# Up projections of three feed-forward blocks: from eight full products to seven of half size

## Chip, core and metric

One NeuronCore of one Trainium2 chip runs the whole program. The metric is the device time of one execution in microseconds (us); the kernel before has a median of 2261.13 us over 3 runs (2261.12 to 2262.95). In the profile PE is TensorE (its weight loads are listed apart, as PEld), DVE is VectorE, ACT is ScalarE, POOL is GpSimd, and SP is the queue that issues most transfers.

## What is computed

Two transformer blocks on 512 tokens of width 1024, in float32. Three feed-forward layers (two in the first block, one in the second) have width 2816 = 22 tiles of 128, and the change concerns these:

```python
def swiglu(h, w1, w3, w2):
    return (jax.nn.silu(h @ w1) * (h @ w3)) @ w2

x = x + 0.5 * swiglu(rms_norm(x, norm_ffn1[l]), ffn1_w1[l], ffn1_w3[l], ffn1_w2[l])
...
x = x + 0.5 * swiglu(rms_norm(x, norm_ffn2[l]), ffn2_w1[l], ffn2_w3[l], ffn2_w2[l])
...
h = rmsnorm(x, g_pre_ffn[l])
gu = h @ w_ffn_in[l]
gate, up = gu[..., :D_FF_2], gu[..., D_FF_2:]
x = x + rmsnorm((jax.nn.silu(gate) * up) @ w_ffn_down[l], g_post_ffn[l])
```

Between them stand retention, differential attention, attention over two memories, an mLSTM and a sparse attention, which the change leaves as they are.

## The kernel before, in words

**Precision.** Every float32 operand is split in two exact parts, hi and lo, of the type fp32r: ACT casts to hi (`copy_hi`, L93, or with a gain L94) and DVE subtracts to get lo (`lo`, L98, with a gain L99). A product is three matmuls (`mm3`): hi with hi, hi with lo, lo with hi, all recorded on L109.

**Weights.** `Stream` holds all weights in the order of their use. It loads one [128, 1024] tile ahead on the SP queue into one of four raw buffers (L146), splits it on ACT and DVE, and keeps `AHEAD` = 4 split tiles in front of the one in use. The split tiles, the residual and all large operands come from one pool of 41 buffers of 4 KB a partition (`q`).

**Residual and norm.** The residual x stands transposed, 8 tiles of [128 features, 512 tokens]. As each tile d is finished, `next_x` splits it with the norm's gain (ACT L94, DVE L99) and POOL squares it and adds it up (`Norm.add`, L222 and L226). 1/rms of each token comes later (`Norm.finish`: sums on PE, a power on POOL L251, a broadcast on PE L258 on) and multiplies the results, not the operands.

**Up phase** (`ffn_up`). For each of 22 tiles f the gate and the up weight (key order gate, up) each take 8 chunks of the width times 3 matmuls of 512 columns. `evac` takes the two results out of PSUM: DVE multiplies gate by 1/rms (L287), ACT applies silu (L288), DVE multiplies up by 1/rms (L290) and by the gate (L291), and the result is split (L93, L98). In the third block (`second_mix`) the residual becomes ready in two halves of 256 tokens (`resid`, `resid2`), and the first two tiles f are computed half by half.

**Down phase.** `ffn_down` goes output tile by output tile: 22 chunks times 3 matmuls of 512 columns. The third block's is `ffn_out`, with the tokens on the partitions.

The kernel is written in a layer that traces instructions and puts them in order for each engine by a planner; every engine then works through its own queue in that order, with semaphores between them. Lines that the steps below touch: L93, L94, L98, L99 (splits), L109 (matmul), L146 (weight load), L215 (sum of squares in the third block), L222, L226 (sums of squares), L251 (power), L287 to L291 (`evac`), L1651, L1716, L1725 (residual adds).

## Time and profile before

| | |
|---|---|
| median of 3 runs | 2261.13 us |
| span of the profiled execution | 2260.1 us |
| PE busy (matmuls) | 2229.0 us, 99% |
| PEld busy (weight loads, beside PE) | 1846.7 us, 82% |
| DVE busy | 1261.5 us, 56% |
| ACT busy | 850.9 us, 38% |
| POOL busy | 340.9 us, 15% |
| share of the chain that ended last: PE, DVE, ACT, POOL | 89%, 5%, 2%, 1% |
| bytes read and written | 224.9 MB, mean 100 GB/s |

The profile is of one execution, whose span runs from the first to the last instruction. The "chain that ended last" is followed back from the last instruction, at each step to what released it. A matmul's busy time holds its way through the array and overlaps the next one's, so what one costs is read from a long run of equal ones, as length by count. In the timeline, neighbours of one kind are merged into one row with their count.

### The profile page before, as it was taken

Reading aid. Unit: us, or ns where it says so; the run is one execution under the profiler, and the core shown is the slowest. Engines: PE = TensorE matmul, PEld = TensorE weight load, DVE = VectorE, ACT = ScalarE, POOL = GpSimd, SP = SyncE. Lnnn points to the kernel's source line nnn. Section 1 sums busy time; section 2 is a strip of 40 time slices with the busy share of each in tenths; the row PEclk is TensorE's granted clock in tenths of the full one; section 3 lists DMA queues with packets and bytes.
Section 4 is the critical chain, followed back from the end, with each engine's and each line's share of the span. In section 5 each row is a group of like instructions: output and inputs, shape, how many; then the busy total and the mean of one; then the engine's idle time right before and its main releaser. Section 6 shows DMA issues by size and latency. Waiting matters only on the chain.

```text
span 2260.1 us, 27814 instructions
## 1 busy us (share of the span) xinstructions
PE 2229.0 (99%) x10730; PEld 1846.7 (82%) x10730; DVE 1261.5 (56%) x2063; ACT 850.9 (38%) x1483; POOL 340.9 (15%) x392
## 2 busy tenths in 40 slices
PE   8999999999999999999999999999999999999998
PEld 6888888888888888888888878887777798888887
DVE  7444434556866655444345955736888757544422
ACT  4222223545344523222223543315666643332320
POOL 3000011301233030000230000213334104000000
PEclk9999999999999999999999999999999999999999
DMA  5332324122333322333224132531111451222321
GB/s 173 104 101 94 102 79 137 53 94 80 125 123 103 103 94 98 105 96 96 94 93 147 58 107 93 173 121 58 57 47 57 147 180 57 94 94 94 128 87 38
DMA packets 73292, 224.92 MB, mean 100 GB/s; under 512 B 8388, under 2 KB 11204, under 8 KB 73160
## 3 DMA queue, kind: packets, MB, share of 16 engines
q1 hardware_dynamic: 72584, 222.10, 30.5%
q8 instruction: 84, 1.38, 0.2%
q10 hardware_dynamic: 576, 1.05, 0.1%
q14 instruction: 48, 0.39, 0.1%
HBM read 210.01 MB, written 13.11 MB: 99 GB/s over the span
## 4 chain that ended last, share of the span: by engine, by line
PE 89%; DVE 5%; ACT 2%; issue 2%; POOL 1%; DMA 1%; SPq 0%; DVEq 0%; POOLq 0%; ACTq 0%
PE ps L109 87%; PE ps L112 2%; DVE q L98 1%; ACT q L1456 1%; POOL hr L251 1%; DVE nx L1454 1%; DVE q L99 0%; ACT q L93 0%; DMA q<-in_xT_dram 0%; DVE q L1354 0%; DVE hn L424 0%; POOL q L1461 0%; ACT q L885 0%; DMA raw<-in_w_k_dram 0%; DVE b L428 0%
## 5 line engine op out<-in xcount | busy, mean ns | idle before, releaser
L109 PE MATMUL ps<-q,q 128*128 128x512 f32 (+3 forms) x9744 | 2160.7, 382 | 13.1 <-ACT q L94 6.2
L109 PEld LDWEIGHTS ps<-q,q 128*128 128x128 f32 x9744 | 1743.2, 189 | 349.5 <-issue 6.6
L98 DVE TENSOR_TENSOR q<-raw,q 128x1024 fp32r<-128x1024 f32 (+2 forms) x381 | 471.3, 1260 | 145.1 <-ACT q L93 71.7
L93 ACT CAST q<-raw 128x1024 fp32r<-128x1024 f32 (+2 forms) x381 | 372.1, 1008 | 168.0 <-PE ps L109 90.6
L93 ACT CAST q<-b 128x512 fp32r<-128x512 f32 (+2 forms) x94 | 56.7, 613 | 362.3 <-DVE b L291 316.2
L222 POOL TENSOR_TENSOR b<-q 128x512 f32<-128x512 f32 (+1 forms) x56 | 56.0, 1003 | 764.8 <-DVE q L1651 324.6
L290 DVE TENSOR_TENSOR b<-ps,b 128x512 f32<-128x512 f32 x44 | 30.4, 690 | 163.8 <-PE ps L109 163.8
L98 DVE TENSOR_TENSOR q<-b,q 128x512 fp32r<-128x512 f32 (+2 forms) x94 | 64.6, 695 | 63.6 <-ACT q L93 62.9
L226 POOL TENSOR_TENSOR b<-b,b 128x512 f32<-128x512 f32 (+1 forms) x70 | 95.2, 1365 | 4.2
L1461 POOL TENSOR_SCALAR q<-q,nr 128x128 f32<-128x128 f32 (+3 forms) x128 | 71.9, 568 | 143.4 <-DVE nr L1459 116.2
L1456 ACT ACTIVATE q<-ps,nx 128x128 f32<-128x128 f32 (+3 forms) x128 | 67.4, 531 | 56.2 <-DVE nx L1454 31.0
L94 ACT ACTIVATE q<-q,gains 128x512 fp32r<-128x512 f32 (+1 forms) x48 | 30.3, 650 | 152.4 <-DVE q L1651 71.8
L112 PE MATMUL ps<-ident,q 128*128 128x128 f32 x512 | 80.8, 274 | 3.5 <-POOL q L1461 2.3
L98 DVE TENSOR_TENSOR q<-ps,q 128x512 fp32r<-128x512 f32 x112 | 74.1, 682 | 11.3 <-ACT q L93 10.9
L288 ACT ACTIVATE b<-b 128x512 f32<-128x512 f32 x66 | 41.2, 630 | 102.9 <-DVE b L287 102.8
L112 PEld LDWEIGHTS ps<-ident,q 128*128 128x128 f32 x512 | 61.8, 140 | 20.7 <-POOL q L1461 7.8
L93 ACT CAST q<-ps 128x512 fp32r<-128x512 f32 x112 | 62.7, 593 | 16.7 <-PE ps L109 11.6
L99 DVE SCALAR_TENSOR_TENSOR q<-q,gains,q 128x512 fp32r<-128x512 f32 (+1 forms) x48 | 47.7, 1013 | 17.4 <-ACT q L94 17.4
L1454 DVE TENSOR_REDUCE nx<-ps 128x1 f32<-128x384 f32 (+3 forms) x96 | 56.0, 583 | 0.0
L290 DVE TENSOR_TENSOR b<-ps,rb 128x512 f32<-128x512 f32 x22 | 15.2, 689 | 73.1 <-PE ps L109 73.1
L251 POOL TENSOR_TENSOR sr<-ss,mhalf 128x4 f32<-128x4 f32 x8 | 8.1, 1008 | 297.6 <-DVE ss L1088 192.9
L251 POOL TENSOR_TENSOR or<-ov,mhalf 128x1 f32<-128x1 f32 x4 | 2.2, 547 | 335.5 <-DVE ov L1994 335.5
(244 smaller groups left out, 1118.3 us busy)
## 6 DMA issues: line engine op xcount, KB each, us to landing
raw<-in_ffn_w_dram SPq DMA_DIRECT2D x118, 512.0 KB, 4.0
raw<-in_w_ffn_in_dram SPq DMA_DIRECT2D x44, 512.0 KB, 4.3
raw<-in_w_gm_dram SPq DMA_DIRECT2D x24, 512.0 KB, 3.6
raw<-in_w_ffn_down_dram SPq DMA_DIRECT2D x22, 512.0 KB, 3.6
raw<-in_w_out_dram SPq DMA_DIRECT2D x16, 512.0 KB, 4.2
raw<-in_ffn_w_dram SPq DMA_DIRECT2D x16, 384.0 KB, 3.1
raw<-in_w_mk_dram SPq DMA_DIRECT2D x8, 512.0 KB, 3.8
raw<-in_w_mv_dram SPq DMA_DIRECT2D x8, 512.0 KB, 4.5
```

The lines of the kernel that those rows point to most:

```text
L93: return self.nc.scalar.copy(out, in_)
L98: return self.nc.vector.tensor_sub(out, in_, hi.bitcast(F32))
L99: return self.nc.vector.scalar_tensor_tensor(out, in_, gain, hi.bitcast(F32), op0=ALU.mult, op1=ALU.subtract)
L109: return self.nc.tensor.matmul(out, a, b, start=start, stop=stop)
L112: return self.nc.tensor.transpose(out, in_, self.ident[:n, :n])
L222: k.nc.gpsimd.tensor_tensor(t, x, x, op=ALU.mult)
L226: k.nc.gpsimd.tensor_tensor(self.acc, self.acc, t, op=ALU.add)
L288: nc.scalar.activation(h, h, AF.Silu)
L290: nc.vector.tensor_mul(u, pb, rb)
L1454: nc.vector.tensor_reduce(mx, s.rearrange("p j b t -> p b j t"), axis=AX.XY, op=ALU.max, negate=True)
L1456: nc.scalar.activation(pr[b][:, :n], s[:, :, c, :], AF.Exp, bias=mx[:, c : c + 1], accum_out=sm[:, c : c + 1])
L1461: nc.gpsimd.tensor_scalar(pr[b][:, :n], pr[b][:, :n], r[:, c : c + 1], 1.0, op0=ALU.mult, op1=ALU.mult)
```

## The change

The matrix product of one pair of f tiles (2n, 2n+1) is cut in two along f, along the width (even and odd chunks of 128) and along the tokens (two halves of 256). Of the eight products of quarters, seven products of sums and differences take the place (Winograd's form of Strassen's scheme). Each has 4 chunks, 2 weights and 3 matmuls of 256 columns.

- Weights: POOL forms four sums of [128, 512] for each of the two weights of a pair (`_sums`); ACT and DVE split f1, both pairs of sums (1024 columns each) and the odd half of f2 (512). The raw buffers go from 4 to 6, the pool of large ones from 41 to 39.
- Moving operands (`Operands`): each pair of residual tiles is multiplied by its gain on ACT, split, and DVE forms four differences of [128, 256], which are split too.
- Products (`UpPairs`): seven for a pair, into three PSUM banks, in the order of `up_steps`. ACT copies three of the partial results out, DVE adds three others and multiplies by 1/rms, ACT applies silu, and POOL multiplies gate and up. The result is kept unsplit.
- Down: `split_g` splits the result tile by tile. `ffn_down` computes the first four output tiles side by side, chunk by chunk, with weights laid out for it, and the last four as before.
- The residual is not kept during the up phase: it is read again from memory (`xT`, `x3d`, `x6d`) by transfers on the ACT queue.

```diff
-        self.qp = pool("q", 41)
+        self.qp = pool("q", 39)
...
-    RAW = 4
+    RAW = 6
     AHEAD = 4
...
+    def _sums(self, n):
...
+        f1, f2 = (t.rearrange("p (k c) -> p k c", c=P) for t in d[key][:2])
+        t = k.q([P, 2, 4, P])
+        eng = nc.gpsimd
+        if what == "s12":
+            eng.tensor_tensor(t[:, 0], f2[:, 0::2], f2[:, 1::2], op=ALU.add)
+            eng.tensor_tensor(t[:, 1], t[:, 0], f1[:, 0::2], op=ALU.subtract)
+        else:
+            eng.tensor_tensor(t[:, 0], f1[:, 0::2], f2[:, 0::2], op=ALU.subtract)
+            eng.tensor_tensor(t[:, 1], f1[:, 1::2], d[key][2][:, 1], op=ALU.subtract)
+        d[key].append(t)
+
+    def _pair_split(self, n):
...
+        if what == "a22":
+            f2 = d[key][1].rearrange("p (k c) -> p k c", c=P)
+            t = k.q([P, 2, 4, P], F32R)
+            k.split(t[:, 0], t[:, 1], f2[:, 1::2])
+            del d[key]
+            return t[:, 0], t[:, 1]
+        t = d[key][2 if what == "s12" else 3].rearrange("p a k c -> p (a k c)")
+        h, l = k.q([P, 1024], F32R), k.q([P, 1024], F32R)
+        k.split(h, l, t)
+        return h, l
...
+    SUMS = 2
...
+    def prefetch(self, ahead):
+        while self.ns <= min(self.n + ahead, len(self.order) - 1):
+            while self.nsum <= min(self.ns + self.SUMS, len(self.order) - 1):
+                self._sums(self.nsum)
+                self.nsum += 1
+            self._split()
...
+class Operands:
...
+    def first(self, x1, x2, g1, g2):
+        k, c = self.k, slice(0, self.H)
+        b1, b2 = k.half(F32R).rearrange("p (s t) -> p s t", s=2), k.q([P, 2, S], F32R)
+        k.split(b1[:, 0], b1[:, 1], x1[:, c], g1)
+        k.split(b2[:, 0, c], b2[:, 1, c], x2[:, c], g2)
...
+    def second(self, j, x1, x2, g1, g2):
+        z1, z2 = self.gained(x1, g1), self.gained(x2, g2)
+        c = slice(self.H, S)
+        k.split(self.b2[j][:, 0, c], self.b2[j][:, 1, c], z2[:, c])
+        self.sums(z1, z2)
...
+    def both(self, x1, x2, g1, g2):
+        z1, z2 = self.gained(x1, g1), self.gained(x2, g2)
...
+        k.split(b1[:, 0], b1[:, 1], z1[:, : self.H])
+        k.split(b2[:, 0], b2[:, 1], z2)
...
+        self.sums(z1, z2)
...
+    def sums(self, z1, z2):
+        t = k.q([P, 4, H])
+        nc.vector.tensor_sub(t[:, 1], z2[:, H:], z1[:, H:])
+        nc.vector.tensor_add(t[:, 0], z1[:, :H], t[:, 1])
+        nc.vector.tensor_sub(t[:, 2:4], z2.rearrange("p (c t) -> p c t", c=2), t[:, 0:1].to_broadcast([P, 2, H]))
+        h, l = k.q([P, 4, H], F32R), k.q([P, 4, H], F32R)
+        k.split(h, l, t)
...
+def up_steps(n, early):
+    if early:
+        o = [(0, 1), (0, 2), (1, 1), (1, 2), (0, 6), (0, 5), (0, 7), (1, 6), (0, 4), (0, 3), (1, 5), (1, 7)]
     else:
+        o = [(0, 1), (0, 2), (0, 6), (0, 5), (0, 7)]
+    for i in range(2 if early else 1, n):
+        o += [(i, 1), (i - 1, 4), (i - 1, 3), (i, 2), (i, 6), (i, 5), (i, 7)]
+    return o + [(n - 1, 4), (n - 1, 3)]
...
+    LEFT = {1: ("f1", 0), 2: ("f1", 1), 3: ("s34", 1), 4: ("a22", 0), 5: ("s12", 0), 6: ("s12", 1), 7: ("s34", 0)}
+    RIGHT = {1: "b11", 2: "b21", 3: "b22", 4: "t4", 5: "t1", 6: "t2", 7: "t3"}
...
+    def out(self, f, half, z, src):
+        nc.vector.tensor_mul(z, src, self.rb[:, c].unsqueeze(1).to_broadcast([P, 2, 256]))
+        nc.scalar.activation(z[:, 0], z[:, 0], AF.Silu)
...
+        nc.gpsimd.tensor_tensor(self.g[f][:, c], z[:, 0], z[:, 1], op=ALU.mult)
+
+    def take(self, n, num):
+        if num in (1, 6, 7):
+            c[n, num] = self.copy(b[n, "x"])
+        if num == 2:
+            z = c.pop((n, 1))
+            nc.vector.tensor_add(z, z, b[n, "z"])
...
+        if num == 7:
+            z = c.pop((n, 7))
+            nc.vector.tensor_add(z, z, b[n, "y"])
+            self.out(2 * n + 1, 1, z, z)
+        if num == 4:
+            self.out(2 * n + 1, 0, k.b([P, 2, 256]), b.pop((n, "x")))
+        if num == 3:
+            z = c.pop((n, 6))
+            nc.vector.tensor_add(z, z, b.pop((n, "y")))
+            self.out(2 * n, 1, z, z)
...
+            if (n, num) == (0, 6):
+                last = self.finish()
+            if (n, num) == (0, 5):
+                self.rb = last()
...
+def split_g(k, g, f):
+    t = k.q([P, 2, S], F32R)
+    k.split(t[:, 0, :], t[:, 1, :], g[f])
+    g[f] = t
...
 def ffn_down(k, key, g):
+    ps = [k.ps() for _ in range(4)]
+    for f in range(NF):
+        if f == 0:
+            split_g(k, g, 0)
+        if f + 1 < NF:
+            split_g(k, g, f + 1)
+        if f % 2 == 0:
+            w = k.W.next((key, "a", f // 2))
+        for d in range(4):
+            c = slice((f % 2) * 512 + d * P, (f % 2) * 512 + (d + 1) * P)
+            k.mm3(ps[d], w[0][:, c], w[1][:, c], g[f][:, 0, :], g[f][:, 1, :], f == 0, f == NF - 1)
...
+    for d in range(0, KD, 2):
+        first[d // 2]()
+        next_pair(x, ops, d, G["norm_ffn1"], norm)
+    x.clear()
+    g = UpPairs(k, ("ffn1_w1", "ffn1_w3"), ops, norm.finish).run()
     for d in range(KD):
+        x.append(k.half())
+        nc.scalar.dma_start(x[d], aps["xT"][d])
```

## Rows read from the trace of the kernel before

**Rows 1.** The page: busy time by engine; shares of the chain that ended last.
```profile
PE 2229.0 (99%) x10730; PEld 1846.7 (82%) x10730; DVE 1261.5 (56%) x2063; ACT 850.9 (38%) x1483; POOL 340.9 (15%) x392
...
PE 89%; DVE 5%; ACT 2%; issue 2%; POOL 1%; DMA 1%; SPq 0%; DVEq 0%; POOLq 0%; ACTq 0%
```

**Rows 2.** Timeline of PE (start, length, operation, shapes, count): long runs of each width.
```profile
2134.76 110.55 PE L109 MATMUL ps<-q,q 128*128 128x512 f32 x487
...
1862.60 20.39 PE L109 MATMUL ps<-q,q 128*128 128x256 f32 x168
...
1891.80 13.44 PE L109 MATMUL ps<-q,q 128*128 128x256 f32 x110
```

**Rows 3.** Groups by shape (busy us, mean ns of one | idle before): weight loads.
```profile
L109 PEld LDWEIGHTS ps<-q,q 128*128 128x128 f32 x9744 | 1743.2, 189 | 349.5 <-issue 6.6 <-DVE q L99 6.5 <-ACT q L94 6.2
```

**Rows 4.** A stretch of the first up phase: PE, PEld, DVE, ACT, POOL busy, clock, DMA.
```profile
150.00:200.00 50.00, 50.00 (x222) 41.39 (x222) 24.40 (x29) 15.76 (x20) 0.00 (x0) 1.00 0.30 95
```

**Rows 5.** Groups by shape: DVE, ACT and POOL operations of the up phases and norms.
```profile
L98 DVE TENSOR_TENSOR q<-raw,q 128x1024 fp32r<-128x1024 f32 x341 | 434.2, 1294 | 131.8 <-ACT q L93 68.7 <-PE ps L109 50.5 <-issue 10.8
...
L291 DVE TENSOR_TENSOR b<-b,b 128x512 f32<-128x512 f32 x66 | 45.5, 692 | 7.0 <-ACT b L288 1.1
...
L93 ACT CAST q<-raw 128x1024 fp32r<-128x1024 f32 x341 | 348.3, 1049 | 147.8 <-PE ps L109 81.1 <-issue 17.5 <-DMA raw<-in_ffn_w_dram 13.4
...
L226 POOL TENSOR_TENSOR b<-b,b 128x512 f32<-128x512 f32 x42 | 71.7, 1715 | 2.4
...
L226 POOL TENSOR_TENSOR b<-b,b 128x256 f32<-128x256 f32 x28 | 23.5, 840 | 1.7
```

**Rows 6.** Timeline of POOL while the first residual tiles are prepared.
```profile
10.97 1.49 POOL L222 TENSOR_TENSOR b<-q 128x512 f32<-128x512 f32 x1
12.42 1.73 POOL L226 TENSOR_TENSOR b<-b,b 128x512 f32<-128x512 f32 x1
14.11 1.22 POOL L222 TENSOR_TENSOR b<-q 128x512 f32<-128x512 f32 x1
15.29 1.46 POOL L226 TENSOR_TENSOR b<-b,b 128x512 f32<-128x512 f32 x1
...
24.14 1.49 POOL L222 TENSOR_TENSOR b<-q 128x512 f32<-128x512 f32 x1
25.71 2.14 POOL L226 TENSOR_TENSOR b<-b,b 128x512 f32<-128x512 f32 x1
```

**Rows 7.** Timeline of DVE in the same stretch.
```profile
9.79 3.21 DVE L99 SCALAR_TENSOR_TENSOR q<-q,gains,q 128x512 fp32r<-128x512 f32 x2
12.93 2.68 DVE L98 TENSOR_TENSOR q<-raw,q 128x256 fp32r<-128x256 f32 x2
...
21.51 3.22 DVE L99 SCALAR_TENSOR_TENSOR q<-q,gains,q 128x512 fp32r<-128x512 f32 x2
24.65 4.28 DVE L98 TENSOR_TENSOR q<-raw,q 128x1024 fp32r<-128x1024 f32 x2
```

**Rows 8.** Groups by shape: two DVE operations that run beside POOL's sums of squares.
```profile
L99 DVE SCALAR_TENSOR_TENSOR q<-q,gains,q 128x512 fp32r<-128x512 f32 x32 | 34.3, 1085 | 16.8 <-ACT q L94 16.8
...
L1716 DVE TENSOR_TENSOR q<-ps,q 128x512 f32<-128x512 f32 x8 | 5.5, 686 | 13.9 <-PE ps L109 13.9
```

**Rows 9.** Timeline of PE at the three entries of the feed-forward layers.
```profile
6.21 0.79 PE L109 MATMUL ps<-q,q 128*128 128x512 f32 x1 [6.21 <-ACT q L94]
...
23.09 9.87 PE L109 MATMUL ps<-q,q 128*128 128x512 f32 x35 [2.63 <-DVE q L99]
...
769.70 65.91 PE L109 MATMUL ps<-q,q 128*128 128x512 f32 x290
...
1886.55 0.58 PE L109 MATMUL ps<-ones,b 128*128 128x1 f32 x4 [3.56 <-DVE b L215]
```

**Rows 10.** Timeline: 1/rms between its sums and its broadcast, second layer.
```profile
836.67 1.02 POOL L251 TENSOR_TENSOR nr<-nv,mhalf 128x4 f32<-128x4 f32 x1 [13.77 <-DVE nv L243]
837.73 0.87 DVE L258 TENSOR_SCALAR b<-ident,nr 128x128 f32<-128x128 f32 x4 [1.13 <-POOL nr L251]
```

More of the change, by code (lines that the diff above doesn't have):

```diff
@@ L106, in split, with mm @@
             self.tc.keep_in_program_order(b)
-    def mm(self, out, a, b, start, stop):
-        return self.nc.tensor.matmul(out, a, b, start=start, stop=stop)
+    def mm(self, out, a, b, start, stop, skip=False):
+        return self.nc.tensor.matmul(out, a, b, start=start, stop=stop, skip_group_check=skip)
     def tr(self, out, in_, n=P):
@@ L133, in __init__ @@
         self.n = 0
+        self.nsum = 0
+        self.pairs = {}
     def add(self, key, src, split=True):
@@ L138, in _dma @@
     def _dma(self):
+        while self.nd < len(self.order) and self.order[self.nd][1] is None:
+            self.nd += 1
         if self.nd < len(self.order):
@@ L147, in _dma @@
             self.raw[self.nd] = t
+            split = self.order[self.nd][2]
+            if isinstance(split, tuple) and split[2] == 0:
+                split[0][split[1]] = [t]
             self.nd += 1
@@ L152, in _split @@
             k = self.k
+            key, src, split = self.order[self.ns]
+            if isinstance(split, tuple) and split[2] != 0:
+                self.hl[self.ns] = self._pair_split(self.ns)
+                self.ns += 1
+                if split[2] == "a22":
+                    self._dma()
+                return
             if self.ns >= self.nd:
                 self._dma()
-            key, src, split = self.order[self.ns]
             t = self.raw.pop(self.ns)
@@ L191, in start @@
                 for d in range(0, KD, 2)]
+    SUMS = 2
     def next(self, key):
-        while self.ns <= min(self.n + self.AHEAD, len(self.order) - 1):
-            self._split()
+        self.prefetch(self.AHEAD)
         assert self.order[self.n][0] == key, (key, self.order[self.n][0])
@@ L346, in next_x, with next_pair @@
     norm.add(x[d])
+def next_pair(x, ops, d, gain, norm):
+    ops.both(x[d], x[d + 1], gain[:, d : d + 1], gain[:, d + 1 : d + 2])
+    norm.add(x[d])
+    norm.add(x[d + 1])
 def weave(main, fill, rate):
@@ L360, in weave, with up_order @@
     return fill
+def up_order(W, keys, srcs, early):
+    seen = set()
+    for n in range(NF // 2):
+        W.pairs[n, keys] = {}
+    for n, num in up_steps(NF // 2, early):
+        what = UpPairs.LEFT[num][0]
+        if (n, what) in seen:
+            continue
+        seen.add((n, what))
+        for key, src in zip(keys, srcs):
+            raw = {"f1": lambda: src[2 * n], "s12": lambda: src[2 * n + 1]}.get(what, lambda: None)()
+            W.order.append(((key, n, what), raw, (W.pairs[n, keys], key, 0 if what == "f1" else what)))
 def units(k, specs, xs, first=None):
@@ L1713, in tile_block @@
     del mem2
-    xs, norm = [], Norm(k)
+    ops, norm = Operands(k), Norm(k)
+    x3d = dr.tile([KD, P, S], F32, name="x3d")
     for d, p in out_proj(k, "mo", cat, list(range(KD))):
         nc.vector.tensor_add(x[d], p, x[d])
-        next_x(k, x, xs, d, G["norm_ffn2"][:, d : d + 1], norm)
-    g = ffn_up(k, ("ffn2_w1", "ffn2_w3"), xs, norm.finish)
-    del xs
+        if d % 2 == 1:
+            next_pair(x, ops, d - 1, G["norm_ffn2"], norm)
+        nc.scalar.dma_start(x3d[d], x[d])
+    x.clear()
+    g = UpPairs(k, ("ffn2_w1", "ffn2_w3"), ops, norm.finish).run()
+    del ops
+    for d in range(KD):
+        x.append(k.half())
+        nc.scalar.dma_start(x[d], x3d[d])
     gc = k.const([P, KD], "gc")
@@ L1767, in second_order @@
         W.add(("wo2", d), a["w_out_2"][d])
-    for f in range(NF):
-        W.add(("gate", f), a["w_ffn_in"][f])
-        W.add(("up", f), a["w_ffn_in"][NF + f])
+    up_order(W, ("gate", "up"), (a["w_ffn_in"][0:NF], a["w_ffn_in"][NF : 2 * NF]), True)
     for f in range(NF):
@@ L1893, in second_mix @@
         x.append(t)
-    xs = [k.q([P, 2, S], F32R) for d in range(KD)]
+    ops = Operands(k)
+    x6d = dr.tile([KD, P, S], F32, name="x6d")
     rbf = k.rb
     norms = []
-    ws = [k.W.next(("wo2", d)) for d in range(KD)]
+    ws = []
+    for d in range(KD):
+        k.W.AHEAD = min(Stream.AHEAD, KD - 1 - d)
+        ws.append(k.W.next(("wo2", d)))
     halves = (slice(0, 256), slice(256, 512))
@@ L1935, in second_mix @@
         product(1, d)
+        if d > 4:
+            k.W.prefetch(d - 5)
+    k.W.AHEAD = Stream.AHEAD
     del ws
@@ L1953, in second_mix @@
     xt = []
+    for d in range(KD):
+        x.append(k.half())
+        nc.scalar.dma_start(x[d], x6d[d])
     for t in range(NT):
@@ L1980, in ffn_out @@
             chunk(t, f, w)
+    for f in range(NF - last + 1, NF):
+        split_g(k, g, f)
     ws = [k.W.next((key, f)) for f in range(NF - last, NF)]
```

222 lines of the change are left out of this document (162 added, 60 removed).

## Prediction

> **What bounds the kernel now.** I read the page first. PE is busy for 99% of the span and carries 89% of the chain that ended last; DVE is at 56%, ACT at 38%, POOL at 15% [rows 1]. So the sum starts with what a matmul costs. The timeline shows long runs without a gap. Two runs of 512 columns, of 487 and 290 matmuls, last 110.55 and 65.91 us [rows 2, 9]: the 197 matmuls between them cost 44.64 us, 0.2267 us each, and the drain of the last falls out. Two runs of 256 columns, of 168 and 110, last 20.39 and 13.44 us: 58 in 6.95 us, 0.120 us each [rows 2]. Half the columns cost 53%, not 50%, and that is already in these steps. A weight load takes 0.189 us in the rows, longer than a step of 0.120 us [rows 3], yet the run of 168 kept its step, so the loads overlap. In an up phase DVE works 24.4 of 50 us, ACT 15.8, and POOL nothing [rows 4]. The reader should keep that zero in mind: the change fills POOL.
>
> **PE's gain.** Before, a pair of f tiles takes 2 tiles x 2 weights x 8 chunks x 3 = 96 matmuls of 512: 21.76 us. After, 7 products x 2 weights x 4 chunks x 3 = 168 of 256: 20.16 us. That is 1.60 us a pair, 52.8 us for 33 pairs. In the third layer two tiles run at 256 columns already, 192 x 0.120 = 23.04 instead of 21.76 us, which goes too: 54.1 us in all. The down phases keep their 528 matmuls each.
>
> **What the pair costs the other engines.** Per pair and weight, ACT and DVE split 3.5 tiles of 1024 columns instead of 2, and POOL makes 4 sums of 512. Results: DVE has 4 operations of 512 with an operand in PSUM (three adds, one product) and 3 with both in SBUF; POOL has 4 products of 256; ACT has 3 copies and 4 silus. ACT: 7 casts at 1.05 us [rows 5] and some 3.5 us of the rest, 11 of 20 us, free. DVE by its rows, some of which hold waits: 7 x 1.29 + 7 x 0.69 = 13.9 us [rows 5]; POOL by its rows: 8 x 1.72 + 4 x 0.84 = 17.1 us [rows 5]. Each alone fits into 20.16 us. Together they may not.
>
> **DVE and POOL take turns.** The timeline shows the two engines in one stretch [rows 6, 7]; compare the ends (start plus length). DVE's pair of 512-column splits ends at 13.00, POOL's operation before at 12.46: 0.54 later. The next POOL operation ends at 14.15, 1.15 after DVE. POOL's next ends at 15.33 and DVE's at 15.61, 0.28 later (256 columns); then POOL at 16.75, 1.14 later. So it goes on: DVE 24.73, POOL 25.63, 0.90 later (a square); at the end POOL 27.85 and DVE 28.93, 1.08 later (1024 columns). Neither advances while the other does: DVE holds the turn for 0.28, 0.55 or 1.08 us, POOL for 1.14 us (sum of two, 512) or 0.90 (square, 512), without a gap between turns. That is why the same DVE split of 512 has a mean of 1.085 us, while an add with one operand in PSUM, beside the same POOL work, keeps 0.686 [rows 8].
> The Trainium skill says this in "SBUF — State Buffer", section "Who interferes with whom": a DVE instruction with two SBUF inputs contends with a POOL one that reads SBUF, the pair of ports is held exclusively, and an instruction with one SBUF input doesn't contend. Here the trace agrees. The rule speaks against the change, whose new POOL work is all of the contending kind.
>
> **Steady state.** Turns per pair. DVE: 6 x 1.08 (f1 and two sums of each weight) + 2 x 0.55 (a22) + 3 x 0.55 (1/rms) = 9.2 us. POOL: 8 x 1.14 + 4 x 0.57 (half of 512) = 11.4 us. Sum 20.6 us, over PE's 20.16. If the lead of the prefetch covers it the excess is 0; if every DVE turn waits for a full POOL turn and its PSUM operations come on top, 9.2 + 11 x 0.95 + 4 x 0.69 = 22.4 us. I take 20.9, near 20.6, since the rows show turns without gaps: 0.74 us over PE for 30 pairs (the first of each layer is in its entry) = +22 us (0 to +67).
>
> **First layer's entry.** PE has done 72 matmuls, 16.3 us of work, when its run from 23.09 ends at 32.96 [rows 9] (72 are those recorded from the row at 6.21 to this one): 16.5 us lost so far. Before, step by step, a residual tile of 512 was enough for PE to go on. After, products 1 and 2 of the first pair (5.76 us) need b1 and b2, but product 6 needs the differences of all 8 tiles. Per two tiles DVE then has 8 turns: five of 256 (two weight pieces, b1, two differences), two of 512, one of 1024 = 3.6 us, 14.3 for all. Beside them stand POOL's 11 sums of squares after 10.97 (6 x 1.14 + 5 x 0.90 = 11.3 us; the first and the last in [rows 6]), the first four weight sums (4.6) and their two splits (2.2). From 9.8 us, DVE's first row there [rows 7]: 9.8 + 32.4 = 42.2; half of product 6 follows, 43.6 us, with 8.64 us of PE's work done: 35 lost, 18 more than before. If DVE never waited, its own 21.2 us give +7; with the next four sums in front as well +23. I take +18, since both queues are full there [rows 6, 7].
>
> **Second layer's entry.** Before, PE runs through it without a gap [rows 9]. The output projection gives 43.5 us of cover (192 x 0.2267) and products 1 and 2 another 5.8. Turns: 8 weight splits 8.6, four pairs of residual tiles at 3.0, sums of squares 8 x 0.90 + 7 x 1.14 = 15.2, the pair's first weights 9.0: 45 us, just covered. What is late is the chain after the last tile: add, gain, differences, cast, split, some 7 to 11 us with turns, against 6.9 us: +4 (0 to +8).
>
> **Third layer's entry.** The second half of the tokens comes only after product 1 of the second pair, and product 6 needs its differences. DVE: per two tiles seven turns of 256, one of 512, one of 1024, 3.6 us, 14.3 in all; POOL 8 squares and 7 sums of 256, 7.6 us. With 1.5 us for ACT's casts in the chain 23.4 us, against 4.0 us of PE work that doesn't need them: +19 (+12 if some of POOL's come late, +26 with the weights' turns). The 3.56 us that PE waits at 1886.55 for the norm [rows 9] I leave.
>
> **The rest.** The power and the broadcast's factors take 1.9 us [rows 10]; the new cover is product 5, 2.88 us, and the power queues behind POOL's sums: +2 for three layers (0 to +6). The splits moved into the down phases: 2 of 0.69 us in 5.44 us of PE (24 x 0.2267), hidden by DVE's idle half; if the first one is late, up to +2.5 a layer. The reload of x on the ACT queue is due after 60 us of down phase; queued behind it are ACT's casts: 0 taken, its price is in the upper bound.
>
> **Sum.** 2260.1 - 54.1 + 22 + 18 + 4 + 19 + 2 = 2271 us of span. The median lies 1.0 us over the span: 2272 us, slower by 0.5%. All lower ends: -54.1 + 0 + 7 + 0 + 12 + 0 = 2226. All upper ends: -54.1 + 67 + 23 + 8 + 26 + 6 + 7.5 = 2345.
>
> **Rivals.** *The gain stays* (faster): PE sets the pace. It decides where the losses stay under 54 us: the prefetch is ahead by four split tiles and two sums, six of a pair's eight, some 15 of its 20 us, and each entry's pause lets POOL and DVE run ahead. Price: steady state +8, entries at their lower ends +19, rest +2: 2236 us. Against it speaks that 20.6 is over 20.16. *The queues block each other* (slower still): each engine works in a fixed order, so a cast that waits for a late POOL sum holds up the PSUM copy behind it, and PE waits for its bank. Decides once POOL falls behind by more than the lead. At 22.4 us a pair and my entries: 2317 us. The Trainium skill's rule in "SBUF — State Buffer", same section, that the ports are held for a whole instruction, would lengthen the turns in the same way; the rows give the shorter ones. *The step isn't halved* (the change doesn't do what it says): loads of 0.189 us show, 1848 x 0.189 against 239.4 us, over 100 us a layer. The Trainium skill, "TensorE: Matmul & The Clock Gate", Part 3, section "The mechanism", says that loads overlap matmuls only when row groups differ, which they don't here; the 168 in a row at 0.120 us speak against it.
>
> **How the numbers follow.** The measurement can tell 0.2%, 4.5 us, from no change. Chances: my forecast (2256 to 2295) 0.48, of which 0.12 lie within 0.2%; the gain stays 0.33; the queues block 0.16; the step isn't halved 0.03. Faster 0.33, same 0.12, slower 0.55. The faster case and the blocking one are as far as 8 in 10 reaches: 2230 to 2318; the forecast's own range is 2256 to 2295.
>
> **What would show it.** Right: runs of 256 columns at 0.120 us; in up phases POOL over half busy where it was zero, L98 on 1024 columns well over 1.29 us, PE gaps released by DVE or ACT; PE idle before product 6 in the first and third layer. Wrong: up phases of 222 us without gaps, or first matmuls of product 6 that start by 30 us.

## Result: 2468.6 us, 9.2% slower

| | before | after |
|---|---|---|
| median | 2261.15 us, 4 runs (2261.12 to 2262.95) | 2468.6 us, 4 runs (2467.26 to 2471.76) |
| ratio, 95% interval | | 1.0916 [1.0901, 1.0932] |
| span of the profiled execution | 2260.1 us | 2467.4 us |
| mean granted clock of TensorE | 0.998 | 0.956 |

The forecast was 2272 us with a range of 2230 to 2318. The side is right, the size is far off, and most of the loss sits in a term that the forecast had with the other sign (the table near the end). The page of after, busy time and chain, answers to [rows 1]:

```profile
PE 2263.5 (92%) x13010; PEld 1988.1 (81%) x13010; DVE 1635.1 (66%) x2270; ACT 1037.1 (42%) x1810; POOL 941.6 (38%) x788
...
PE 58%; POOL 15%; DVE 11%; issue 10%; ACT 5%; DMA 1%; SPq 0%; POOLq 0%; DVEq 0%; ACTq 0%
```

PE fell from 89% to 58% of the chain that ended last, and POOL rose from 1% to 15%, though POOL is busy for only 38% of the span. Where the time went is read by stage. Each stage ends with the start of its last DVE or POOL operation of one line (last product of gate and up, last residual add); the third column belongs to an experiment below.

| stage (us) | before | after | sums on DVE |
|---|---|---|---|
| up phase 1, from the start | 258.7 | 335.2 | 271.3 |
| down phase 1 | 118.9 | 118.9 | 119.3 |
| middle, to the first residual add of the output projection | 408.4 | 412.3 | 410.8 |
| output projection | 33.3 | 41.0 | 39.4 |
| up phase 2 | 242.1 | 291.5 | 228.7 |
| down phase 2 | 118.8 | 118.8 | 119.6 |
| mixing of the second block, to its residual | 683.4 | 683.5 | 683.8 |
| residual and up phase 3 | 266.3 | 327.4 | 278.4 |
| down phase 3 | 130.2 | 138.8 | 139.6 |

So 187.0 of the 207.3 us lie in the up phases. A period of the first up phase, in PE's rows of the timeline (start, length, operation, count, idle before and its releaser), answers to [rows 2]:

```profile
152.29 22.89 PE L109 MATMUL ps<-q,q 128*128 128x256 f32 x168 [4.27 <-ACT b L463]
179.46 22.94 PE L109 MATMUL ps<-q,q 128*128 128x256 f32 x168 [4.28 <-ACT b L463]
206.68 3.57 PE L109 MATMUL ps<-q,q 128*128 128x256 f32 x15 [4.28 <-ACT b L463]
```

A pair takes 27.2 us where the forecast had 20.9 and PE's own work is 20.16. In each period PE stops once for 4.28 us, until ACT's copy of a product out of PSUM (L463), and the row of its 168 matmuls takes 22.9 us, where the row of 168 in [rows 2] takes 20.39. The stretch that answers to [rows 4] shows why the second (columns: PE, PEld, DVE, ACT, POOL busy, granted clock, DMA):

```profile
150.00:200.00 50.00, 43.43 (x318) 43.23 (x319) 36.18 (x29) 19.09 (x29) 32.93 (x23) 0.86 0.21 68
```

The mean granted clock is 0.86 there, against 1.00 before. Cut finer, it stands at the lower level, 1.2 GHz, for 6.8 us from the last microsecond of each gap on (the gap before 179.46 here), and at the higher one for the rest of the period:

```profile
178.44:185.24 6.80, 5.78 (x27) 5.78 (x28) 5.12 (x6) 2.50 (x4) 3.83 (x2) 0.50 0.48 157
185.27:205.70 20.43, 17.13 (x143) 16.92 (x142) 15.17 (x11) 7.86 (x12) 14.87 (x11) 1.00 0.18 52
```

The groups that answer to [rows 5], and three groups of new POOL work:

```profile
L98 DVE TENSOR_TENSOR q<-raw,q 128x1024 fp32r<-128x1024 f32 x281 | 399.8, 1440 | 99.9 <-ACT q L93 59.0 <-issue 26.5 <-PE ps L109 12.4
L98 DVE TENSOR_TENSOR q<-q,q 128x1024 fp32r<-128x1024 f32 x144 | 251.6, 1764 | 93.0 <-ACT q L93 75.1 <-POOL q L211 12.7 <-PE ps L109 3.3
L474 POOL TENSOR_TENSOR q<-b 128x256 f32<-128x256 f32 x132 | 124.4, 947 | 280.4 <-ACT b L471 280.4
...
L210 POOL TENSOR_TENSOR q<-raw,raw 128x512 f32<-128x512 f32 x66 | 114.8, 1739 | 0.2
L207 POOL TENSOR_TENSOR q<-raw 128x512 f32<-128x512 f32 x66 | 114.8, 1757 | 2.4 <-DMA raw<-in_w_ffn_in_dram 2.4
```

The reader should set the third line beside the last two. The sums (L207, L210) start without a wait, back to back; the 132 products of gate and up (L474) stand in POOL's queue ahead of them and wait 280.4 us for ACT's silu. POOL waits for PE's results, then sums in a burst, and the burst is late for PE. The timeline over the rest of the period shows the whole circle:

```profile
190.99 0.69 DVE L484 TENSOR_TENSOR b<-b,ps 128x512 f32<-128x512 f32 x1 [1.53 <-PE ps L109]
191.71 0.69 DVE L470 TENSOR_TENSOR b<-b,b 128x512 f32<-128x512 f32 x1
192.44 0.42 ACT L471 ACTIVATE b<-b 128x256 f32<-128x256 f32 x1 [2.53 <-DVE b L470]
...
193.00 0.75 POOL L474 TENSOR_TENSOR q<-b 128x256 f32<-128x256 f32 x1 [2.28 <-ACT b L471]
193.69 3.53 POOL L207 TENSOR_TENSOR q<-raw 128x512 f32<-128x512 f32 x2
...
197.19 3.98 POOL L208 TENSOR_TENSOR q<-q,raw 128x512 f32<-128x512 f32 x2
...
201.12 1.74 POOL L210 TENSOR_TENSOR q<-raw,raw 128x512 f32<-128x512 f32 x1
...
202.82 2.24 POOL L211 TENSOR_TENSOR q<-raw,q 128x512 f32<-128x512 f32 x1
...
205.09 1.04 ACT L93 CAST q<-q 128x1024 fp32r<-128x1024 f32 x1 [2.84 <-POOL q L211]
206.04 0.58 ACT L463 COPY b<-ps 128x512 f32<-128x512 f32 x1
206.68 1.23 PE L109 MATMUL ps<-q,q 128*128 128x256 f32 x4 [4.28 <-ACT b L463]
```

From 179.46 PE works for 11.4 us up to product 2. DVE adds and multiplies (L484, L470), ACT applies silu (L471), and at 193.00 POOL makes the period's fourth product. Only now come its next sums; six of the eight run from 193.69 to 205.06. ACT's cast of the last of these six (L93) stands in ACT's queue ahead of the copy of product 7 (L463), and PE's next product adds into that bank. 11.5 us of PE and its drain, 2.0 of DVE and ACT, 12.1 of POOL, 1.6 of ACT: 27.2, one pair.

Two other costs lie inside this circle and make it longer. The six sums take 11.4 us; alone they would take some 7.9 (1.32 us from one to the next in the run with the turns by themselves, below), so some 3.5 us are DVE's turns. And PE's 11.5 us hold the stretch at the lower clock, some 2.5 us. My estimate from these figures is a circle of some 21 us without either.

### The profile page after: what moved, and what is told of

Same layout as the page of the kernel before. It is cut to its first block, busy times and chain, and to the rows that moved or that the text cites. A ratio compares the mean times of both kernels' runs of the same rounds, so it can differ in the third digit from the quotient of the medians.

```text
span 2467.4 us, 33549 instructions
## 1 busy us (share of the span) xinstructions
PE 2263.5 (92%) x13010; PEld 1988.1 (81%) x13010; DVE 1635.1 (66%) x2270; ACT 1037.1 (42%) x1810; POOL 941.6 (38%) x788
## 4 chain that ended last, share of the span: by engine, by line
PE 58%; POOL 15%; DVE 11%; issue 10%; ACT 5%; DMA 1%; SPq 0%; POOLq 0%; DVEq 0%; ACTq 0%
PE ps L109 56%; POOL q L211 4%; DVE q L98 4%; POOL q L208 3%; POOL q L210 3%; ACT q L93 2%; PE ps L112 2%; DVE b L470 2%; POOL q L207 1%; POOL q L474 1%; DVE nx L1721 1%; ACT q L1723 1%; DVE b L484 1%; DMA raw<-in_ffn_w2a_dram 1%; ACT b L463 1%
## 5 line engine op out<-in xcount | busy, mean ns | idle before, releaser
L109 PE MATMUL ps<-q,q 128*128 128x256 f32 (+2 forms) x12024 | 2190.7, 345 | 178.8 <-ACT b L463 102.9
L109 PEld LDWEIGHTS ps<-q,q 128*128 128x128 f32 x12024 | 1881.4, 199 | 407.8 <-ACT b L463 109.0
L98 DVE TENSOR_TENSOR q<-raw,q 128x1024 fp32r<-128x1024 f32 (+3 forms) x379 | 533.4, 1432 | 132.3 <-ACT q L93 75.8
L98 DVE TENSOR_TENSOR q<-q,q 128x1024 fp32r<-128x1024 f32 (+1 forms) x212 | 296.4, 1418 | 145.9 <-ACT q L93 127.9
L93 ACT CAST q<-raw 128x1024 fp32r<-128x1024 f32 (+3 forms) x379 | 344.1, 937 | 114.2 <-PE ps L109 85.3
L93 ACT CAST q<-q 128x1024 fp32r<-128x1024 f32 (+1 forms) x212 | 190.0, 911 | 346.4 <-POOL q L211 142.0
L474 POOL TENSOR_TENSOR q<-b 128x256 f32<-128x256 f32 x132 | 124.4, 947 | 280.4 <-ACT b L471 280.4
L471 ACT ACTIVATE b<-b 128x256 f32<-128x256 f32 x132 | 54.9, 417 | 200.5 <-DVE b L470 200.5
L211 POOL TENSOR_TENSOR q<-raw,q 128x512 f32<-128x512 f32 x66 | 138.6, 2099 | 0.0
L208 POOL TENSOR_TENSOR q<-q,raw 128x512 f32<-128x512 f32 x66 | 118.0, 1805 | 0.6
L207 POOL TENSOR_TENSOR q<-raw 128x512 f32<-128x512 f32 x66 | 114.8, 1757 | 2.4 <-DMA raw<-in_w_ffn_in_dram 2.4
L210 POOL TENSOR_TENSOR q<-raw,raw 128x512 f32<-128x512 f32 x66 | 114.8, 1739 | 0.2
L463 ACT COPY b<-ps 128x512 f32<-128x512 f32 x99 | 57.3, 579 | 60.7 <-PE ps L109 60.3
L98 DVE TENSOR_TENSOR q<-ps,q 128x512 fp32r<-128x512 f32 x112 | 74.2, 683 | 11.1 <-ACT q L93 10.7
L93 ACT CAST q<-ps 128x512 fp32r<-128x512 f32 x112 | 62.6, 592 | 16.8 <-PE ps L109 11.7
```

The lines of the kernel that those rows point to most:

```text
L93: return self.nc.scalar.copy(out, in_)
L98: return self.nc.vector.tensor_sub(out, in_, hi.bitcast(F32))
L109: return self.nc.tensor.matmul(out, a, b, start=start, stop=stop, skip_group_check=skip)
L207: eng.tensor_tensor(t[:, 0], f2[:, 0::2], f2[:, 1::2], op=ALU.add)
L208: eng.tensor_tensor(t[:, 1], t[:, 0], f1[:, 0::2], op=ALU.subtract)
L210: eng.tensor_tensor(t[:, 0], f1[:, 0::2], f2[:, 0::2], op=ALU.subtract)
```

## Experiments

Theory T: DVE and POOL take turns, which sets the rate (20.6 to 22.4 us a pair). Rival Q: the fixed queues close the circle above.

**The products off POOL** (2377.9 us).

```diff
-        nc.gpsimd.tensor_tensor(self.g[f][:, c], z[:, 0], z[:, 1], op=ALU.mult)
+        nc.vector.tensor_mul(self.g[f][:, c], z[:, 0], z[:, 1])
```

> One edit: the products of gate and up (4 of 256 columns a pair) go from POOL to DVE, so POOL's queue holds weight sums alone and ACT's queue keeps its order. Theory Q (fixed queue order): the sums stand behind products that wait for PE, so a period of 27.2 us is a loop through PE, DVE, ACT, POOL; without the products the sums start as soon as the weights land, PE's 4.56 us gap and the clock's fall go. Then a pair is near 20.2 to 21 us and the whole 2467 - 30 x 6 to 7, about 2260 to 2290 us. Theory T (the turns of DVE and POOL alone set the pace): the turns change by only 4 x (0.28 - 0.57) = -1.2 us a pair, so 2430 us or more.

Neither number came out. A pair takes 22.8, 22.4 and 23.2 us in the three layers (26.9, 26.8, 25.3 after), 90 us less in all. In the first two layers this takes off more than half of a period's loss, in the third less; the pairs stay 2.2 to 3.0 us over PE's work.

**No sums at all** (2282.0 us).

```diff
-        t = d[key][2 if what == "s12" else 3].rearrange("p a k c -> p (a k c)")
+        t = d[key][1 if what == "s12" else 0]
```

> The weight sums are left out: the splits of the two sum tiles read the loaded tiles f2 and f1 instead, so the number of splits, loads and matmuls stays and the result isn't the product. Both theories: POOL is near idle in the up phases, nothing waits for it, a pair costs PE's 20.16 us and the clock stays up. What is left over the kernel before is then the entries: 2261 - 54 + 41 (my three entries) + 2 = about 2250 us; if the entries come from POOL's sums too, 2215 to 2230.

The pairs take 20.16 us in all three layers: products, copies and seven-product bookkeeping don't hold PE by themselves. But the total is 21 us above before, where 54 us less PE work should have brought it under. The entries and the rest cost some 75 us, not 43, so neither total expected came out. By the reckoning of the table near the end the entries alone are 26, 8 and 25 us here, without a single weight sum on POOL.

**The sums on DVE** (2292.9 us).

```diff
-        eng = nc.gpsimd
+        eng = nc.vector
```

> The weight sums (8 of 512 a pair) go from POOL to DVE; POOL keeps the products. DVE by its own durations is then 13.5 + 8 x 0.69 = 19.0 of 20.16 us a pair, with turns lost only to the four products. Theory Q: the sums no longer stand behind the products, but DVE's queue has them in front of the adds that free PSUM; some gap stays, 22 to 24 us a pair, 2320 to 2380 us. Theory T: turns fall from 20.6 to 9.2 + 2.3 with the sums off POOL, a pair near 20.5 us, 2270 us.

One row of PE holds seven pairs:

```profile
109.81 145.36 PE L109 MATMUL ps<-q,q 128*128 128x256 f32 x1210
```

That is 0.1201 us each, without a gap. DVE now does the work of both and is busy for 43.8 of 50 us, at full clock:

```profile
150.00:200.00 50.00, 50.00 (x419) 50.00 (x418) 43.80 (x56) 24.83 (x38) 18.62 (x12) 1.00 0.26 87
```

This takes off 175 us: with the sums off POOL nothing of the steady state's loss is left. The pairs are near theory T's number; the total fits neither. The edit takes away both the circle and the turns with the sums, so by itself it doesn't part the two. The up phase of the second layer is 13.4 us shorter than before, with 6.1 more in the output projection in front of it; the first and third are 12 longer (table above, third column).

**The price of the turns by itself.** A kernel with nothing but one pair's DVE and POOL operations, six pairs at a time, in four stretches.

> This kernel leaves the whole computation out; it runs nothing but the operations that DVE and POOL have for one pair of f tiles, six pairs at a time, with no order between the two engines, in four stretches: DVE's alone, POOL's alone, both side by side, and POOL's eight sums beside 16 DVE additions with one operand in PSUM. Theory T (the two engines take turns whenever both read only SBUF; terms of the forecast): DVE alone 9.2 + 4 x 0.69 = 12.0 us a pair, POOL alone 8 x 1.14 + 4 x 0.57 = 11.4, both together 20.6 to 22.4 a pair (124 to 134 us for six), and in the last stretch no turns, 11 to 12 a pair. Rival Q (the engines only wait for each other through the fixed order of the queues of the real kernel): both together stay near the longer of the two alone, 12 to 14 a pair (72 to 84 us). If turns cost more than the operations alone, which the 22.4 to 23.2 us a pair of the kernel with the products on DVE suggests, the third stretch is over 22.4 a pair.

The four stretches (DVE alone, POOL alone, both, POOL's sums beside DVE additions with one operand in PSUM) from the first operation to the last (columns: DVE, ACT, POOL busy, granted clock, DMA), and two rows from the end of the third:

```profile
5.92:81.12 75.20, 75.03 (x93) 0.52 (x1) 0.00 (x0) 1.00 0.00 0
81.90:159.58 77.68, 0.00 (x0) 0.57 (x1) 75.89 (x72) 1.00 0.00 0
161.80:290.15 128.35, 112.36 (x92) 0.61 (x1) 120.20 (x72) 1.00 0.00 0
290.95:355.43 64.48, 60.81 (x89) 0.58 (x1) 60.79 (x48) 1.00 0.00 0
...
253.68 30.16 POOL L50 TENSOR_TENSOR s<-raw 128x512 f32<-128x512 f32 x19
283.87 0.69 DVE L57 TENSOR_TENSOR w<-z,s 128x512 f32<-128x512 f32 x1 [15.89 <-POOL s L50]
```

Alone DVE needs 75.2 us, 1.2 of them for two additions that join the stretches: 12.3 a pair. POOL needs 77.7 / 6 = 12.9. Together they take 128.3 / 6 = 21.4. The third stretch isn't side by side throughout: DVE's queue has the joining addition (L57) ahead of its last five splits, so DVE stands idle for 15.9 us while POOL finishes, and those five come after POOL's end at 283.84. Up to there it is 122.0 / 6 = 20.3 us with the five missing. So T's sum (20.6) lies within what was measured, 20.3 to 21.4, but it is a bound on the rate, and the kernel ran at 27.2. In the last stretch neither engine slows the other: 48 sums in 64.5 us, the 1.3 us each that they take alone.
The Trainium skill, "SBUF — State Buffer", section "SBUF: two separate sides", has whichever of the two operations starts first hold the pair of ports for the whole instruction. By the lengths of the first two stretches, less four additions with a PSUM operand at some 0.6 us, that would be an estimate of 12.3 - 2.4 + 12.9 = 22.8 us a pair. The measured 21.4 at most is less; I take it that what an instruction has of its own at start and end overlaps the other engine's turn. The Trainium skill, on the same page, section "Who interferes with whom", lets a DVE instruction with at most one SBUF input run beside POOL, and the last stretch agrees.

**The clock.** 36 dummy matmuls of 256 columns on PE after product 1, from the third pair on, to fill the gap.

```diff
+        for i in range(36):
+            k.mm(p[:, 0], bh[:, 0:128], bh, i == 0, i == 35, True)
```

> As the changed kernel, with 36 matmuls of 256 columns that nothing needs, 4.3 us, on PE at the place of its gap (after product 1 of each pair from the third on); nothing else changes. If the gap of 4.56 us lets the granted clock fall and that costs the other 2.5 us of a pair's 27.2, then PE is busy through the gap, the clock stays at its upper level and a pair takes 24.7 us: 27 pairs x 2.5 = about 65 us less, near 2400 us. If the clock has another cause, or the filler delays the loop, 2467 us or up to 2580.

2475.5 us. In layers 1 and 2 a pair takes 24.8 us instead of 26.9 and 26.8, and the time at the lower clock falls from 219 to 112 us.

```profile
173.18 20.42 PE L109 MATMUL ps<-q,q 128*128 128x256 f32 x168
193.44 4.48 PE L109 MATMUL ps<-q 128*128 128x256 f32 x36
197.93 20.42 PE L109 MATMUL ps<-q,q 128*128 128x256 f32 x168
```

PE has no gap left here and sets these 24.8 us itself, so the half clock was at least 2 us of a period; the rows of 168 matmuls, 22.9 us there and 20.4 here, give 2.5. In layer 3 a pair takes 28.1 instead of 25.3: there PE still waits for the copy out of PSUM, and I take it that the dummies delay the results, and with them the circle.

**More lead.** From the kernel with the products on DVE: one raw buffer more, one large buffer less, sums three entries ahead.

```diff
-    RAW = 6
+    RAW = 7
...
-    SUMS = 2
+    SUMS = 3
```

> The kernel with the result products on DVE, whose pairs took 22.4 to 23.2 us where the turns alone make some 20, with one raw buffer more (7), one large one less (38) and sums three entries ahead instead of two. Theory L (what remains there is lead: a cast that waits for a late sum stands in front of a copy out of PSUM): 20.2 to 21.2 us a pair, total 2310 to 2345. Rival R (what remains is the rate of DVE and POOL together): pairs stay at 22.4 or more, total 2370 to 2385.

2375.4 us; 22.1, 22.2 and 23.3 us a pair. This follows rival R's number, not its reason: in a period of the kernel with the products on DVE POOL stands idle for 10.8 us before its sums.

```profile
166.10 2.72 POOL L207 TENSOR_TENSOR q<-raw 128x512 f32<-128x512 f32 x2 [10.82 <-DVE b L470]
```

So it isn't the rate either. I take it that the sums wait for a large buffer, since this kernel had one fewer and gained nothing. The page of the kernel with the products on DVE fits that: more than half of the idle time before these sums ends with PE's matmuls, which give back the weights that they have read.

```profile
L207 POOL TENSOR_TENSOR q<-raw 128x512 f32<-128x512 f32 x66 | 100.6, 1535 | 266.1 <-PE ps L109 142.9
```

It is argued, not shown, and stays open.

**One part alone: the split in the down phase,** with the full products of before in all layers.

```diff
-        nc.vector.tensor_mul(u, u, h)
-        t = k.q([P, 2, S], F32R)
-        k.split(t[:, 0, :], t[:, 1, :], u)
+        t = k.half()
+        nc.vector.tensor_mul(t, u, h)
         g.append(t)
```

> One part alone: full products of before in all three layers, but their result is kept unsplit and split in the down phase, which makes its first four output tiles side by side as in the change. The forecast put this part at 0 to 2.5 us a layer: 2261 to 2268. The up phases lose 22 casts and 22 subtractions each, which are beside PE's work, so they stay at 217 us. If it is over 2270, the down phases hold a cost that the forecast missed.

2265.3 us beside 2262.4 of before. This part is as cheap as forecast; 1.1 us of it are in down phase 3.

**Seven products in the second layer only,** sums on DVE, first with five raw buffers (and 40 large ones), then with the change's six (and 39), then with layers 1 and 3 as before throughout.

```diff
-        up_order(W, (gate, up), (aps[gate], aps[up]), False)
+        if n + 1 in NEW:
+            up_order(W, (gate, up), (aps[gate], aps[up]), False)
+        else:
+            for f in range(NF):
+                W.add((gate, f), aps[gate][f])
+                W.add((up, f), aps[up][f])
```

> Seven products only in the second layer, with the weight sums on DVE; layers 1 and 3 use the full products of before with their result kept unsplit and the residual kept in place. From the run with the sums on DVE: that layer's up phase is 14.6 us shorter with its entry inside it, the output projection in front of it 5.4 longer, the down phases some 2 each: 2260.9 - 14.6 + 5.4 + 2 to 6 = 2254 to 2258, the first of these runs under the kernel before. Theory T (turns were the steady-state cost, the entries take the rest, and layers 1 and 3 have the dear entries): 2252 to 2258. Rival E (the entries' cost comes from buffers and order in any layer): 2262 or more.

2285.8 us, ratio 1.0102 [1.0085, 1.0119]: rival E's side, but the trace shows another cause. The second layer's period is 22.5 us, with several waits of 0.3 to 0.7 us for splits in each:

```profile
902.94 8.42 PE L110 MATMUL ps<-q,q 128*128 128x256 f32 x68 [0.29 <-DVE q L99]
912.04 0.74 PE L110 MATMUL ps<-q,q 128*128 128x256 f32 x4 [0.68 <-ACT q L94]
913.30 11.87 PE L110 MATMUL ps<-q,q 128*128 128x256 f32 x96 [0.52 <-DVE q L99]
925.45 8.42 PE L110 MATMUL ps<-q,q 128*128 128x256 f32 x68 [0.28 <-DVE q L99]
```

> The last run had seven products in the second layer only, but five raw buffers instead of the change's six and 40 large buffers instead of 39; its second layer took 22.5 us a pair. This one has six and 39, nothing else differs. Theory B (the missing raw buffer makes each split just in time): the second layer comes back to 20.0 us a pair and to 228 us between the last residual tile and the last silu, 30 us less than in that run: 2254 to 2258, faster than before by 0.2 to 0.4%. Rival (the third layer or the full products of layers 1 and 3 run badly with fewer buffers): over 2262.

2260.3 us, 0.9994 [0.9985, 1.0003]. The second layer's up phase is back at 228.9 us, from 258.6: the sixth raw buffer is worth some 30 us there. The total missed the expectation by 2 us: the middle takes 410.6 us instead of 408.4. That goes with the 39 large buffers or the six raw ones: the kernels with 40 or 41 and fewer raw ones have 408.1 to 408.6 in that stage, those with 39 and six have 410.6 to 412.4. No run parts the two.

> As the run beside it, but layers 1 and 3 split their result in the up phase again and layer 1 has its down phase of before, so that only the second layer is changed. The part alone (result split in the down phase) cost 3 us for three layers, so 2 us less than the run beside it: 2252 to 2256. With 39 large buffers instead of 41 the ends of the up phases of layers 1 and 3 may hold weights back; then it is above the run beside it.

2258.8 us, 0.9986 [0.9977, 0.9995]: 3 us under before, and above the 2252 to 2256 expected; the middle takes 412.3 us here.

**The entries.** First the early order of products in all layers (2293.3 us):

> The kernel with the sums on DVE, but layers 1 and 2 take the order of products that the third layer has: products 1 and 2 of the second pair stand in front of product 6 of the first, 5.76 us more of PE work that doesn't need the differences. Theory E (PE waits at an entry for the differences of the last tiles): layer 1 is 4 to 6 us shorter than in the run with the sums on DVE (its up phase ends at 264 to 266 instead of 269.7), layer 2 takes 3 to 5 off, the total is 2282 to 2286. Rival (the entries are bound by DVE's whole queue, which now has the second pair's weights in front as well): no gain or a loss, 2290 to 2297.

The first layer gains 2 us, the second loses 1: the rival's total. More cover from PE alone hardly helps here; that DVE's whole queue is the reason is the rival's account, not shown. Then full products for the first pair, so that the differences are formed beside 22 us of PE work that doesn't need them:

```diff
+    def whole(self, bank, w, half=None, ks=None):
+        for j in range(KD // 2) if ks is None else ks:
...
+            for h in (0, 1) if half is None else (half,):
+                b = (self.b1, self.bx)[h][j]
+                k.mm3s(bank[:, h * H : (h + 1) * H], *we, b[:, 0], b[:, 1], j == 0 and (h == 0 or half is not None), False)
...
+            k.mm3s(bank[:, c], *wo, self.b2[j][:, 0, c], self.b2[j][:, 1, c], False, j == KD // 2 - 1)
```

> Sums on DVE, and the first pair of f tiles of each layer by full products (four results of 8 chunks, which need the split residual only), seven products from the second pair on; the differences of the residual tiles are formed while the first pair runs. In the third layer the residual is transposed for the last step while the first pair runs, and stored, instead of read back at the end. Theory E (the dear part of the entries is PE's wait for the differences, since 20 us of the 75 to 86 us of entries and exits come from product 6): ten pairs of each layer keep 1.6 us each, 48 us in all, the first pairs cost 0.6 us each for the even chunks in two halves, the down phases cost the 3 us of the part alone, and each entry keeps some 2 to 5 us of DVE's extra work: 2261 - 48 + 2 + 3 + 10 = 2228, between 2222 and 2242. Rival D (the entries are bound by DVE's whole load, which is the same here, or the differences come late for the second pair): over 2255.

2260.3 us, 0.9991 [0.9981, 1.0000], 33 us under the kernel with the sums on DVE, but 32 over the number expected. One row holds 11.75 us of that:

```profile
1920.46 3.68 PE L112 MATMUL ps<-ident,q 128*128 128x128 f32 x16 [11.75 <-ACT q L2283]
```

The transposes that I had put into the third entry wait for a bank, whose copy comes on ACT behind three casts of the entry, each of which waits for DVE's differences: the fault of the change once more, made by me.

With the read back at the end of the third up phase, as in the change:

> As the run beside it, but the residual is read back at the end of the third layer's up phase and transposed there, as in the change. In the run with the sums on DVE PE lost some 11 us at that place, with a wait of 4.6 us for the read in front of the transposes. If that is what the read back costs, this run is 8 to 12 us above the run beside it; if the cost there came from the splits, the two are within 3 us.

2263.9 us, only 4 above the run beside it, whose own transposes were badly placed: the third up phase is 9.2 us shorter here, down phase 3 13.2 longer. It is 29 us under the kernel with the sums on DVE, by the full first pairs and the later differences alone. Down phase 3 is where the read back shows: with the sums on DVE, PE waits for it between the phases,

```profile
2154.54 6.18 PE L112 MATMUL ps<-ident,q 128*128 128x128 f32 x28 [4.62 <-DMA q<-x6d]
```

and that phase takes 139.6 us, 130.2 before.

With the transposes four at a time between later products:

```diff
+            if n > 1 and self.aside:
+                self.aside.pop(0)()
```

> The run with full products for the first pair stood at 2260.3 instead of the 2228 expected. Its trace shows one gap of 11.75 us on PE in the third layer: the transposes of the residual, put in the entry, wait for a PSUM bank whose copy is behind the entry's casts on ACT; after it the clock is granted at half for 17 us. Here the same 32 transposes go four at a time between the products of the second seven-product pair and the next. Theory P (that wait is the loss): 12 us of gap and some 8 of half clock go: 2238 to 2244, faster than before by 0.8 to 1.1%. Rival (the third entry is held by DVE and ACT in any case): 2252 or more.

2254.7 us, 0.9962 [0.9948, 0.9976]: 5.6 us less, a third of the 16 to 22 that theory P expected, and on its rival's side. The gap of 11.75 us is gone, but behind the first pair PE now waits five times for ACT and DVE, 5.6 us in all. The longest of these waits:

```profile
1925.57 0.80 PE L109 MATMUL ps<-q,q 128*128 128x256 f32 x2 [2.40 <-ACT q L93]
```

And with products of the next pair ahead in the first layer:

```diff
+        o = [(1, 1), (1, 2), (2, 1), (2, 2), (1, 6), (1, 5), (1, 7), (2, 6), (1, 4), (1, 3), (2, 5), (2, 7)]
```

> As the run beside it, and in the first layer products 1 and 2 of the next pair stand in front of the first product 6, which waits 5.6 us in three gaps there, with half clock for 7 us after it. Theory E: 4 to 8 us less than the run beside it (2232 to 2238). Rival (DVE's load in that entry is what counts, and the next pair's weights add to it): within 2 us of it, as the same order brought 2 us in the earlier run.

**2252.6 us, 0.9960 [0.9947, 0.9972],** 2 us under the run beside it, as its rival said, and within the spread of the two (2252.3 to 2254.7 against 2251.7 to 2256.2); it is the lowest median of all. By stages it has 256.7 us for up phase 1, 33.3 and 231.8 for the second projection and up phase, 273.9 and 122.2 for the third up and down phase. Beside before (258.7, 33.3, 242.1, 266.3, 130.2) the second layer keeps 10.3 of its 16 us, the third 0.4 with its down phase, and the middle takes 2.4 more. The first keeps 2: PE still waits four times for differences and copies after its first pair.

```profile
51.74 7.27 PE L109 MATMUL ps<-q,q 128*128 128x256 f32 x58 [1.60 <-DVE q L98]
64.82 0.50 PE L109 MATMUL ps<-q,q 128*128 128x256 f32 x2 [1.14 <-ACT b L475]
66.49 1.92 PE L109 MATMUL ps<-q,q 128*128 128x256 f32 x14 [1.17 <-DVE q L98]
69.91 30.27 PE L109 MATMUL ps<-q,q 128*128 128x256 f32 x250 [1.50 <-DVE q L98]
```

## Why the prediction was wrong, step by step

The sum of the forecast against the stages (periods by layer 26.88, 26.80, 25.28 us, means over the middle pairs; a pair of before 21.76):

| term | forecast | measured |
|---|---|---|
| 30 pairs in steady state, against before | 30 x (20.9 - 21.76) = -26 | 51 + 50 + 35 = +137 |
| three first pairs and the third layer's 256-column tiles | -6 | -6 |
| entries 1, 2, 3 | 18, 4, 19 | 27, 8, 29 |
| the rest (power, split, read back, middle) | 2 | 13 |
| sum | +11 | +207 |

An entry's number is the difference of its up phase less ten periods, with the first pair's own gain put back: 76.5 - 51.2 + 1.6 = 26.9 for the first; the second has the output projection's 7.7 with it, the third 1.3 for its 256-column tiles. The second line is taken over from the forecast, and the last two carry some rounding. Ten middle periods say some too much, since the last two pairs of the first two layers take only 20 to 21 us: counted by PE's matmuls, the thirty pairs after each layer's first take 775 us, 122 more than before. What the first line has too much, 15 us, its third line has too little.

That the side was right is in part luck: the forecast was slower by its entries, while its steady state was to gain 26 us and lost 122. And every sign that it named for being right came (0.120 us a matmul, POOL busy for 32.9 of 50 us, L98 at 1440 and 1764 ns, gaps ended by ACT, PE idle before product 6): none of them measured the period.

- **PE's gain** was right. The step of 0.120 us holds for 1210 matmuls in a row, and the rival that the step isn't halved is out.
- **The turns** were right: 20.6 forecast, 20.3 to 21.4 measured by themselves.
- **The steady state is the step that failed:** "I take 20.9, near 20.6, since the rows show turns without gaps". From the rate of two engines I concluded the pace of the kernel. Its condition, that both always have something to do, was not held against the order of POOL's queue. That queue has four products, which need PE's results, in front of the next eight sums, which PE needs for its next pair. Work of a whole period then stands in one line, and the period is the length of the circle (27.2), not the largest of the engines' sums (21.4 at most). Some 150 of the 196 us by which the forecast missed are here (775 against 30 x 20.9 = 627; 163 by the table's equal periods).
- **The rival "the queues block each other"** named the right kind of fault with a chance of 0.16, and one of its two places: the cast ahead of the PSUM copy on ACT. The rival that the gain stays, with a chance of 0.33, fell by the same step: a lead of six tiles doesn't help where the next sums start only behind the products. The blocking rival missed these products ahead of the sums on POOL, and its price of 22.4 us was that of the turns at their worst. A circle has no such bound; it had to be priced by adding the durations along it, and most of them stood in the rows; what the turns and the clock add inside it did not.
- **The clock** was in no term. It stands at 1.2 GHz for 6.8 us from the last microsecond of each gap shown on; by the run with dummy matmuls that is at least 2 us of a period.
- **The entries** were too small by 23 us (38 by the count of PE's matmuls). That PE waits ahead of product 6 was right, but the turns with POOL's weight sums are the smaller part of the cost: without any of these sums the entries are still 26, 8 and 25 us. What the larger part is made of is shown only for its start. I had priced what DVE does after its first row of before [rows 7]; the change multiplies by the gains on ACT first, six of these operations ahead of the first cast of the residual, and PE's first matmul comes 7 us later than in [rows 9]:

```profile
13.31 1.10 PE L109 MATMUL ps<-q,q 128*128 128x256 f32 x2 [13.31 <-ACT q L93]
```

- **The rest:** the split in the down phase at 0 to 2.5 us a layer was right (3 us in all). The read back "0 taken" was wrong: down phase 3 is 8.6 us longer, 1.1 of them also with the split alone, where PE's transposes stand behind it. The new numbers of buffers, which go with 2 to 4 us in the middle, weren't priced.

## What to carry to other kernels

Where a change gives an idle engine work in both directions, for results and for the next inputs, write down its queue in order and follow one period around all queues: if an operation that waits for this period's result stands in front of one that feeds the next, the period is the sum along that circle, however low each engine's share. Separate the two directions, or put them where nothing waits: here the sums on a busier engine, DVE, cost less than on the idle one. The start of each phase has to be priced as its own circle, too, and the best cure of those tried was to let the first pair use the old method.

## What the runs showed of the hardware

- DVE operations on two SBUF operands and POOL operations on SBUF take turns: 12.3 and 12.9 us of work alone are 20.3 to 21.4 together, and with one operand of DVE's in PSUM there is no loss.
- In each period shown, a gap of 4.28 us on PE goes with 6.8 us of clock at the lower level, 1.2 GHz, from the gap's last microsecond on.
- One raw buffer of 4 KB a partition, five instead of six, took the pair from 20 to 22.5 us, without any engine being fully busy (PE for 92.5, DVE for 80.1 of 100 us).
